# Routed experts on one Trainium2 core: TensorE's order written out unit by unit

## The chip, the cores and the metric

One NeuronCore of a Trainium2 chip runs the whole program. The metric is the device time of one execution in microseconds (us), as the median of several runs; smaller is better. TensorE does the matrix products, VectorE (DVE) and ScalarE (ACT) the elementwise work, GpSimd (POOL) some of it, and SyncE (SP) issues the loads from HBM.

## The reference

The program is a two-layer transformer block followed by a second block with a retention mixer, a delta-rule mixer and a mixture of experts, for 256 tokens of 1024 features in float32. The change is in the last stage alone, the routed experts. Each token picks 8 of 64 experts; expert `e` computes

```
(silu(x @ w_gate[e]) * (x @ w_up[e])) @ w_down[e]        # 1024 -> 256 -> 1024
```

for the tokens that picked it. The outputs, each times its token's weight, are added up per token, the shared expert's output is added, and the sum is normalised and added to x.

## The kernel before

**Units and groups.** The experts are ordered by load. The first 12 places get 128 slots for tokens each, the next 28 get 64, the last 24 get 32 (`TIERS`, L53). A unit is 128 slots: one expert, two or four. A group is two units, 256 slots. There are 16 groups, so 32 units: 12 of one expert, 14 of two, 6 of four. `ORDER` (L55) gives the tiers of the groups: 0, 2, 0, 0, 1, 1, 0, 1, 1, 0, 1, 2, 0, 1, 1, 2. Numbered from 0, units 2, 3, 22, 23, 30 and 31 have four experts, units 0, 1, 4 to 7, 12, 13, 18, 19, 24 and 25 have one.

**What a group and a unit do.** `gather` (L1742) picks a group's tokens with one-hot matrices: one step on VectorE and ScalarE (the one-hot tile `oh` and its bfloat16 copy `ohb`), then four steps of 8 matmul records each (`pm<-oh,tok`), each copied by ScalarE into the tile `xg` (2 buffers). A unit's gate and up products (`pd<-ring,xg`) come in four chunks; chunk `c` uses one tile of weights per expert (128 x 1024 floats, 512 KB). Every float32 product is two records. With one expert the records are 128*128, the whole array; with two or four they are 128*64 or 128*32, so that two or four experts stand side by side in the array's columns (column-tiled). A chunk is 4, 8 or 16 records. After that come the steps of `tail` (L1830): `onehot` (products `pm<-slT,idb` and `pm<-w,ohb`; VectorE makes from them `PT`, the matrix that brings outputs back to tokens, and `wc`, the slots' weights); `act` (`swiglu`, L1873: tanh on ScalarE, three steps on VectorE, the last writes `h`); `trans` (two transposes of `h`, L1858, copied by ScalarE into `hT`); two `down` steps (`pm<-ring,hT`, 4, 8 or 16 records each, column-tiled like gate and up), each split by ScalarE and VectorE into the two parts of `y` (3 buffers). Per group `scatter` (L1892) adds four steps of 4 records (`pm<-y,PT`, whole array), each added to the sum `macc` by VectorE (L1883).

**Weights.** `ring` (L1573) loads each tile of weights on SP's queue into one of 25 buffers (`NRING`, L50). An expert takes 6 loads: 4 of `w_gu`, 2 of `w_ed`. A unit of one, two or four experts takes 6, 12 or 24, the routed experts take 384, and the shared expert's last product takes 2 more beside group 2 (`SHD`, L52; products `pm<-ring,hs`, 16 records). A load waits until a buffer is free, that is until the products of an earlier tile are done.

**Order.** Python issues a chunk of gate and up products, then one or two (four experts: up to three) calls of `pump` (L1786), each of which issues one step of `tail` and one of `gather`. This is the order of priority only. The framework's scheduler, working from its own estimate of times when the program is built, decides the final order on each engine, and on TensorE it may put any product that is ready in front of another. PSUM has three `pd` buffers and four `pm` buffers (L329, L332). `final_rows` (L1954) runs beside the last group; it makes rows for the last norm, and holds one `y` and one `xg` buffer from then on.

Of the kernel before, what the change touches and what calls it, by code (L numbers as in the profile page):

```python
# [28 lines left out]
# ----------------------------------------------------------------- constants (of the shapes alone)  # L29
# [24 lines left out]
# the tiers of the groups of 256 slots, in the order in which they are taken  # L54
# [6 lines left out]
def _consts():  # L61
# [3 lines left out]
    # additive masks, queries on partitions  # L65
# [4 lines left out]
    # [partition t, free i]  # L70
# [4 lines left out]
    # within 32 rows and columns, lower and upper: the second block of a pair of s rows, the first of s columns  # L75
# [30 lines left out]
    # rope rows: 0..31 cos, 32..63 sin (with the sign), twice  # L106
# [40 lines left out]
def _layout(inp):  # L147
# [50 lines left out]
    # second block  # L198
# [34 lines left out]
# ----------------------------------------------------------------- kernel  # L233


class Kern:
# [12 lines left out]
    # -------- streams of instructions: generators that yield where another stream may come in  # L249
# [35 lines left out]
    def mm3(self, out, L, R, n, start=True, stop=True):  # L285
        """out = sum over n k-tiles of L[k]^T R[k]; L, R: (hi, lo) callables of k"""
# [19 lines left out]
    def split(self, hi, lo, src, lo_eng=None):  # L306
        """hi + lo = src exactly, each with at most 12 significant bits"""
# [3 lines left out]
    def wraw(self, src, n):  # L311
        """src [128, n] in DRAM, loaded"""
# [6 lines left out]
    def wload(self, src, n, pre=True):  # L319
        """src [128, n] in DRAM -> hi, lo [128, n]"""  # L320
# [25 lines left out]
    # -------- setup  # L346
# [67 lines left out]
    def t5_bias(self, tp):  # L414
        """bias tiles [128 q, 8 heads, keys] with the masks added"""
# [5 lines left out]
        # differences of neighbouring buckets; bucket 0 keeps its value  # L421
# [4 lines left out]
        # three exact bf16 parts, block-diagonal over the key groups  # L426
# [26 lines left out]
                # ps columns (k, g, h) -> bias[q, h, g * nk + h0 + k]  # L453
# [6 lines left out]
    # -------- 1/sqrt(src * scale + eps), [128, n] for small n  # L460
# [13 lines left out]
    def rows(self, cols, dst):  # L474
        """dst [128, 256] = cols [128, 2] (tokens on partitions) as a row on every partition"""
# [6 lines left out]
    def rstd(self, sqs, n, name, dst=None):  # L482
        """1/sqrt(mean + eps) over the partitions of the [128, 256] tiles sqs: (columns [128, 2], rows [128, 256])"""
# [7 lines left out]
    def rstd_rows(self, sqs, n, tmp):  # L491
        """rows of 1/sqrt(mean + eps) over the partitions, worked out on every partition; tmp [128, 4, 256]"""
# [5 lines left out]
    def add_sq(self, acc, k, x, eng=None, **kw):  # L498
        """acc (+)= x^2, the first k writing it"""
# [10 lines left out]
    # -------- dense products; activations (hi, lo) [128, KT, 256]; calls cb(f, psum [128, n * 256], n)  # L510
# [97 lines left out]
            # output projection (the gates' halves come in here), residual  # L608
# [13 lines left out]
    def ff(self, l, XM, r, fp, res):  # L622
        """x += mlp(x), in two halves of the hidden features; res: the next XG and sums of squares"""
# [31 lines left out]
    def queries(self, l, XG, r, qp):  # L655
        """projections of the sliding-window attention"""
# [22 lines left out]
    def mixer(self, l, XG, Q, mp):  # L679
# [4 lines left out]
        # convolution branch: GLU, then the taps  # L684
# [20 lines left out]
        # sliding-window attention  # L705
# [9 lines left out]
        # latent attention: projections and norms of the latents  # L715
# [25 lines left out]
        # gates (tanh: 2 * sigmoid - 1) and the gated sum of the branches, which takes the first gate's place  # L741
# [15 lines left out]
        def branch(n, Y, f, gate):  # L757
            """outputs f, f + 1 of branch n"""
# [11 lines left out]
        # latent attention  # L770
# [50 lines left out]
        # layer norm over channels, swish  # L821
# [32 lines left out]
    def residual(self, k, X, g, acc, eng=None):  # L854
        """after x^T tile k is final: hi, lo of x*g and its part of the sum of squares"""
# [6 lines left out]
    # ---------------------------------------------------------------- second block  # L862
# [11 lines left out]
    def modulation(self, js, mp):  # L874
        """stream: parts js of the modulation, as columns [128, 8] each; 0, 1 for the context too (columns 48..63)"""
# [39 lines left out]
    def modulated(self, x, r, a, b, X, pool):  # L915
        """hi, lo of x * r * a + b; r rows, a and b columns per k-tile"""
# [6 lines left out]
    def decays(self, pool):  # L923
        """powers of the retention's decays: columns"""
# [8 lines left out]
    def decay_tables(self, pool):  # L933
        """DT [128 j, 4, 128 i], both directions; rows of powers"""
# [14 lines left out]
    def tr4(self, dst, srcs, scale=None):  # L949
        """dst [128, 4, 128] = transposes of four [128, 128] tiles, times scale(i) [128, 1]"""  # L950
# [11 lines left out]
    def rope2(self, dst, ps, f, scale, pool):  # L962
        """dst [128, 2, 256] = rotated ps (two heads), times scale"""
# [8 lines left out]
    def short_conv(self, z, ps, tile0, pool):  # L972
        """z [128, 2, 256] = 2 * silu(conv(ps)) of two channel tiles"""
# [12 lines left out]
    def l2(self, zs, pool, kt, ktok, mul):  # L986
        """z = 2 * silu; kt [128, 4, 256] (channels on partitions) and ktok [128, 2, 4, 128] of the normalised heads, times mul"""
# [12 lines left out]
    def state_features(self, X, base, pool, rope, F):  # L1000
        """stream: the features that feed the states, into the dict F"""
# [27 lines left out]
        # the decay gates first  # L1029
# [14 lines left out]
    def gdn_gates(self, p3, la, be, pool):  # L1044
        """la = -exp(a_log) * softplus(p + dt_bias), be = sigmoid(p)"""
# [6 lines left out]
        # softplus(x) = max(x, 0) + log1p(exp(-|x|)); log1p(e) = 2 atanh(e / (2 + e))  # L1052
# [23 lines left out]
    def retention_kv(self, F, d, n, pool, kv):  # L1076
        """kv [PSUM 128 d, (4, 128 e)] of chunk n, direction d"""
# [989 lines left out]
```

## Time and profile before

| what | value |
|---|---|
| median of 3 runs | 2062.32 us (2062.28 to 2063.19) |
| span of the profiled execution | 2062.9 us |
| TensorE busy / VectorE / ScalarE | 92% / 62% / 38% of the span |
| granted TensorE clock, mean | 0.951 of full speed |
| routed experts' first and last product of a ring tile | 1458.2 and 2048.0 us |
| loads of the ring | 390 of 512 KB |

The profiled execution's own time is its span, 0.6 us above the median of the runs, so the two can be used side by side. A row of a timeline merges neighbouring records of one kind; its time runs from the first start to the last end. Matmuls are pipelined: one record of 512 columns shows some 600 ns from start to end while the next one has long begun. What a run costs is therefore read from the start of one row to the start of the next. Records that work in different columns of the array overlap fully.

### The profile page before, as it was taken

Reading aid. Unit: us, or ns where it says so; the run is one execution under the profiler, and the core shown is the slowest. Engines: PE = TensorE matmul, PEld = TensorE weight load, DVE = VectorE, ACT = ScalarE, POOL = GpSimd, SP = SyncE. Lnnn points to the kernel's source line nnn. Section 1 sums busy time; section 2 is a strip of 40 time slices with the busy share of each in tenths; the row PEclk is TensorE's granted clock in tenths of the full one; section 3 lists DMA queues with packets and bytes.
Section 4 is the critical chain, followed back from the end, with each engine's and each line's share of the span. In section 5 each row is a group of like instructions: output and inputs, shape, how many; then the busy total and the mean of one; then the engine's idle time right before and its main releaser. Section 6 shows DMA issues by size and latency. Waiting matters only on the chain. (4 is left out here: it accounts for less than half of the span.)

```text
span 2062.9 us, 38136 instructions
## 1 busy us (share of the span) xinstructions
PE 1900.5 (92%) x15189; PEld 1512.5 (73%) x15189; DVE 1272.2 (62%) x2464; ACT 786.7 (38%) x1397; POOL 292.4 (14%) x216
## 2 busy tenths in 40 slices
PE   5888999999888999998988998996999999999996
PEld 5787999999787999998987988895645443433432
DVE  7999787887986688578657864487222222222223
ACT  3246555344257555444444433352212121121111
POOL 3433210001334220011131121103000000000000
PEclk9989999999989999999989997896999999999998
DMA  4423556776423567655523522154798988889994
GB/s 160 124 82 113 171 177 201 244 245 200 134 76 106 176 202 228 210 172 172 156 91 96 161 91 65 33 180 186 264 409 305 353 276 304 283 287 409 348 349 197
DMA packets 122149, 414.49 MB, mean 201 GB/s; under 512 B 13936, under 2 KB 14832, under 8 KB 121968
## 3 DMA queue, kind: packets, MB, share of 16 engines
q1 hardware_dynamic: 120528, 409.92, 58.7%
q8 instruction: 120, 1.97, 0.4%
q10 hardware_dynamic: 1440, 2.11, 0.3%
q14 instruction: 61, 0.50, 0.1%
HBM read 410.92 MB, written 1.05 MB: 200 GB/s over the span
## 5 line engine op out<-in xcount | busy, mean ns | idle before, releaser
L283 PE MATMUL pd<-X,whi 128*128 128x256 f32 (+2 forms) x3280 | 639.3, 294 | 19.6 <-DVE X L304 9.8
L283 PEld LDWEIGHTS pd<-X,whi 128*128 128x128 f32 (+2 forms) x3280 | 534.0, 198 | 25.9 <-DVE X L304 11.7
L292 ACT ACTIVATE whi<-raw 128x1024 fp32r<-128x1024 f32 x340 | 356.4, 1051 | 458.7 <-PE pd L283 341.2
L283 PE MATMUL pd<-X,wlo 128*128 128x256 f32 (+2 forms) x1640 | 480.0, 293 | 8.2 <-POOL wlo L295 4.6
L295 DVE TENSOR_TENSOR wlo<-raw,whi 128x1024 fp32r<-128x1024 f32 x286 | 357.5, 1253 | 130.7 <-ACT whi L292 125.7
L283 PEld LDWEIGHTS pd<-X,wlo 128*128 128x128 f32 (+2 forms) x1640 | 324.7, 198 | 12.2 <-POOL wlo L295 6.1
L283 PE MATMUL pd<-ring,xg 128*64 128x512 f32 (+2 forms) x1024 | 284.3, 602 | 0.0
L283 PE MATMUL pd<-H,whi 128*128 128x256 f32 x1024 | 188.4, 286 | 0.3 <-ACT H L292 0.3
L295 DVE TENSOR_TENSOR y<-pm,y 128x512 fp32r<-128x512 f32 x64 | 44.2, 691 | 209.6 <-ACT y L292 209.5
L283 PEld LDWEIGHTS pd<-ring,xg 128*64 128x64 f32 (+2 forms) x1024 | 78.3, 136 | 113.4 <-issue 105.3
L295 POOL TENSOR_TENSOR wlo<-raw,whi 128x1024 fp32r<-128x1024 f32 (+1 forms) x54 | 132.6, 2470 | 197.6 <-ACT whi L292 197.2
L283 PEld LDWEIGHTS pd<-H,whi 128*128 128x128 f32 x1024 | 159.4, 192 | 1.1 <-ACT H L292 0.5
L283 PE MATMUL pm<-ring,hT 128*64 128x512 f32 (+2 forms) x512 | 153.7, 601 | 1.6 <-ACT hT L292 1.6
L304 DVE SCALAR_TENSOR_TENSOR cv<-up,vec,cv 128x256 f32<-128x256 f32 x240 | 148.1, 656 | 0.2
L283 PE MATMUL pd<-H,wlo 128*128 128x256 f32 x512 | 145.2, 284 | 0.4 <-DVE wlo L295 0.4
L304 DVE SCALAR_TENSOR_TENSOR acc<-rawm,sl,acc 128x512 f32<-128x512 f32 x112 | 94.1, 855 | 22.6 <-DMA rawm<-in_w_mod 22.2
L292 ACT ACTIVATE y<-pm 128x512 fp32r<-128x512 f32 (+1 forms) x66 | 39.4, 597 | 171.4 <-PE pm L283 171.4
L283 PEld LDWEIGHTS pd<-H,wlo 128*128 128x128 f32 x512 | 98.1, 192 | 0.8 <-DVE wlo L295 0.8
L283 PEld LDWEIGHTS pm<-ring,hT 128*64 128x64 f32 (+2 forms) x512 | 42.1, 136 | 75.1 <-issue 66.8
L283 PEld LDWEIGHTS pm<-oh,tok 128*128 128x128 f32 x512 | 67.2, 189 | 35.0 <-issue 29.3
L295 POOL TENSOR_TENSOR sqacc<-sqacc,sq 128x256 f32<-128x256 f32 x42 | 37.7, 905 | 366.0 <-ACT sq L292 364.9
L283 PE MATMUL pm<-oh,tok 128*128 128x256 f32 x512 | 87.3, 306 | 1.8 <-DVE oh L295 1.8
(515 smaller groups left out, 2721.6 us busy)
## 6 DMA issues: line engine op xcount, KB each, us to landing
ring<-in_w_gu SPq DMA_DIRECT2D x256, 512.0 KB, 6.8
ring<-in_w_ed SPq DMA_DIRECT2D x128, 512.0 KB, 8.5
raw<-in_w_up SPq DMA_DIRECT2D x64, 512.0 KB, 4.3
raw<-in_w_dn SPq DMA_DIRECT2D x64, 512.0 KB, 4.3
raw<-in_w_g SPq DMA_DIRECT2D x48, 512.0 KB, 3.6
rawm<-in_w_mod SPq DMA_DIRECT2D x96, 256.0 KB, 3.5
raw<-in_w_s SPq DMA_DIRECT2D x32, 512.0 KB, 3.7
raw<-in_w_x SPq DMA_DIRECT2D x32, 512.0 KB, 3.5
```

The costliest lines, as they stand in the source:

```text
L283: return self.nc.tensor.matmul(out, l, r, start=start, stop=stop)
L292: self.nc.scalar.activation(out, in_, f, **kw)
L295: (eng or self.nc.vector).tensor_tensor(out, a, b, op)
L304: self.nc.vector.scalar_tensor_tensor(out, a, s, b, op0, op1)
```

## The change

`experts` gets a new loop, and `tail` is taken apart into methods of the same content (`slots`, `hidden`, `turn`, `down`). The scheduler is told that TensorE's instructions keep the order in which Python issues them (`manual_schedule`); the other engines and SP's queue are scheduled as before. Of each unit first all gate and up products are issued, then what uses the whole array (two steps of the next group's gather, the next unit's `slots`, this unit's transposes, two steps of an earlier group's scatter, each with a step of the shared expert or of `final_rows` if there is one), then the unit's two down products. `slots` moves one unit ahead of where `onehot` stood, and `PT` gets a fifth buffer for that. `final_rows` starts with the last group but one. The remaining hunks take comments and docstrings out; the line numbers stay nearly the same.

```diff
     def experts(self, first):
...
-        nxt = self.gather(*order[0])
-        todo.extend(nxt[1])
-        for g, (j0, n) in enumerate(order):
-            while todo:
-                todo.popleft()()
-            if g == SHD:
-                tail.extend(first)
-            if g == len(order) - 1:
-                tail.extend(self.final_rows())
...
-                for c in range(4):
-                    ws = [self.expert_w("w_gu", self.expert(U, i), c) for i in range(nu)]
-                    for kk in range(2):
...
-                    pump()
-                    if nu == 1 or c % 2:
-                        pump()
-                    if nu == 4:
-                        pump()
-                tail.extend(self.tail(U))
...
+        with self.tc.manual_schedule(engines={mybir.EngineType.PE}):
+            st, steps = self.gather(*groups[0])
+            for f in steps:
+                f()
...
+            group(0, st)
+            self.slots(units[0])
+            for i in range(2 * len(groups)):
+                U = units[i]
+                g, second = divmod(i, 2)
+                if not second and g + 1 < len(groups):
+                    st, steps = self.gather(*groups[g + 1])
+                    group(g + 1, st)
+                    todo.extend(steps)
+                if i == 2 * SHD:
+                    extra.extend(first)
+                if i == 2 * len(groups) - 4:
+                    extra.extend(self.final_rows())
+                self.gate_up(U)
+                self.hidden(U)
+                for _ in range(2 if second else 3):
+                    if todo:
+                        todo.popleft()()
+                if i + 1 < len(units):
+                    self.slots(units[i + 1])
+                self.turn(U)
+                for _ in range(2):
+                    if out:
+                        out.popleft()()
+                    if extra:
+                        extra.popleft()()
+                for hf in range(2):
+                    self.down(U, hf)
+                if second:
+                    out.extend(self.scatter(units[i - 1:i + 1]))
+            while out:
+                out.popleft()()
...
-    def tail(self, U):
...
-            U["PT"] = mp.tile([P, S], F32R, name="PT", tag="PT", bufs=4)
...
+    def slots(self, U):
...
+        U["PT"] = mp.tile([P, S], F32R, name="PT", tag="PT", bufs=5)
```

## Rows read from the trace of the kernel before

**Rows 1.** The page: busy time of TensorE, share of the span, instructions.

```profile
PE 1900.5 (92%) x15189; PEld 1512.5 (73%) x15189; DVE 1272.2 (62%) x2464; ACT 786.7 (38%) x1397; POOL 292.4 (14%) x216
```

**Rows 2.** By window: us; PE, PEld, DVE, ACT, POOL busy; granted clock, DMA share, GB/s.

```profile
1866.00:1920.00 54.00, 52.07 (x236) 20.37 (x234) 14.11 (x34) 8.79 (x17) 0.00 (x0) 1.00 1.03 409
...
1993.00:2036.00 43.00, 38.96 (x230) 14.47 (x227) 12.00 (x30) 7.78 (x15) 0.00 (x0) 1.00 0.97 383
...
1458.00:2049.00 591.00, 581.38 (x2639) 247.65 (x2638) 158.10 (x347) 112.25 (x216) 0.00 (x0) 1.00 0.87 321
```

**Rows 3.** Timeline of TensorE, one two-expert unit: start, us, line, out<-in, records.

```profile
1606.40 1.94 PE L283 MATMUL pd<-ring,xg 128*64 128x512 f32 x8
1608.27 1.20 PE L283 MATMUL pm<-y,PT 128*128 128x512 f32 x4
1609.40 1.94 PE L283 MATMUL pd<-ring,xg 128*64 128x512 f32 x8
1611.27 2.14 PE L283 MATMUL pm<-y,PT 128*128 128x512 f32 x8
1613.33 1.94 PE L283 MATMUL pd<-ring,xg 128*64 128x512 f32 x8
1615.20 0.30 PE L283 MATMUL pm<-slT,idb 64*64 64x256 bf16 x2
1615.43 1.07 PE L283 MATMUL pd<-ring,xg 128*64 128x512 f32 x2
1616.43 0.30 PE L283 MATMUL pm<-w,ohb 128*128 128x2 bf16 x6
1616.66 1.94 PE L283 MATMUL pd<-ring,xg 128*64 128x512 f32 x8
1618.53 0.44 PE L1858 MATMUL pm<-cst,h 128*128 128x128 f32 x2
1618.90 1.50 PE L283 MATMUL pd<-ring,xg 128*64 128x512 f32 x5
```

**Rows 4.** The same timeline: two column-tiled runs, one behind the other.

```profile
1636.61 1.89 PE L283 MATMUL pd<-ring,xg 128*64 128x512 f32 x8
1638.33 1.89 PE L283 MATMUL pm<-ring,hT 128*64 128x512 f32 x8
```

**Rows 5.** Timeline of TensorE, the first group: whole-array products.

```profile
1454.36 3.99 PE L283 MATMUL pm<-oh,tok 128*128 128x256 f32 x32 [1.81 <-DVE oh L295]
1458.18 1.88 PE L283 MATMUL pd<-ring,xg 128*128 128x512 f32 x4
...
1474.90 3.60 PE L283 MATMUL pm<-ring,hT 128*128 128x512 f32 x8
1478.33 1.88 PE L283 MATMUL pd<-ring,xg 128*128 128x512 f32 x4
```

**Rows 6.** Timeline of ScalarE and VectorE: one unit from sums to hidden features.

```profile
1516.89 0.38 ACT L292 ACTIVATE tg<-pd 128x256 f32<-128x256 f32 x1 [2.84 <-PE pd L283]
...
1518.15 0.42 DVE L295 TENSOR_TENSOR h<-tg,pd 128x256 f32<-128x256 f32 x1
...
1520.80 0.39 ACT L292 ACTIVATE hT<-pm 128x256 f32<-128x256 f32 x1 [3.04 <-PE pm L1858]
```

**Rows 7.** Ring tiles: ns min/median/max; idle until (us, times); landing of loads, us.

```profile
L283 PE MATMUL pd<-y,ring x64: 379/379/792, 1428.2 to 1452.2; 128*128 128x256 f32 x64
...
  DMA ring<-in_w_gu: 1.1, 2
...
DMA to landing us min/median/max: 3.5/7.2/12.2
```

**Rows 8.** Timeline of all engines, the end of the last unit.

```profile
2046.68 1.90 PE L283 MATMUL pm<-ring,hT 128*32 128x512 f32 x10
...
2048.62 0.60 ACT L292 ACTIVATE y<-pm 128x512 fp32r<-128x512 f32 x1 [4.59 <-PE pm L283]
2049.25 0.69 DVE L295 TENSOR_TENSOR y<-pm,y 128x512 fp32r<-128x512 f32 x1 [2.67 <-ACT y L292]
```

More of the change, by code (lines that the diff above doesn't have):

```diff
@@ L1780, in experts @@
         tiers = [list(range(a, b, 256 // n)) for (a, n), b in zip(TIERS, [t[0] for t in TIERS[1:]] + [NE])]
-        order = []
+        groups = []
         for i in ORDER:
-            order.append((tiers[i].pop(0), 256 // TIERS[i][1]))
-        todo, tail, pend = deque(), deque(), []
-        def pump():
-            if tail:
-                tail.popleft()()
-            if todo:
-                todo.popleft()()
-        nxt = self.gather(*order[0])
-        todo.extend(nxt[1])
-        for g, (j0, n) in enumerate(order):
-            while todo:
-                todo.popleft()()
-            if g == SHD:
-                tail.extend(first)
-            if g == len(order) - 1:
-                tail.extend(self.final_rows())
-            st = nxt[0]
-            if g + 1 < len(order):
-                nxt = self.gather(*order[g + 1])
-                todo.extend(nxt[1])
-            nu = n // 2
-            for u in range(2):
-                U = {"js": list(range(j0 + u * nu, j0 + (u + 1) * nu)), "st": st, "s0": u * P, "reg": {}, "ps": self.pd()}
-                m = P // nu
-                for c in range(4):
-                    ws = [self.expert_w("w_gu", self.expert(U, i), c) for i in range(nu)]
-                    for kk in range(2):
-                        k = 2 * c + kk
-                        for i, w in enumerate(ws):
-                            s0 = U["s0"] + i * m
-                            self.mm(U["ps"][i * m:(i + 1) * m], st["x"][:, k, s0:s0 + m], w[:, kk * 512:(kk + 1) * 512], k == 0, k == KD - 1)
-                    pump()
-                    if nu == 1 or c % 2:
-                        pump()
-                    if nu == 4:
-                        pump()
-                tail.extend(self.tail(U))
-                pend.append(U)
-                if len(pend) == 2:
-                    tail.extend(self.scatter(pend))
-                    pend = []
@@ L1825, in experts, with group @@
-        while tail:
-            tail.popleft()()
+            groups.append((tiers[i].pop(0), 256 // TIERS[i][1]))
+        with self.tc.manual_schedule(engines={mybir.EngineType.PE}):
+            st, steps = self.gather(*groups[0])
+            for f in steps:
+                f()
+            units = []
+            todo, extra, out = deque(), deque(), deque()
+            def group(g, st):
+                j0, n = groups[g]
+                nu = n // 2
+                for u in range(2):
+                    units.append({"js": list(range(j0 + u * nu, j0 + (u + 1) * nu)), "st": st, "s0": u * P, "reg": {}})
+            group(0, st)
[30 more added lines that the diff above has]
+                out.popleft()()
@@ L1827, in experts, with gate_up @@
         self.o = self.xg().rearrange("p (t k) s -> p t (k s)", t=2)
         self.norm_out()
-    def tail(self, U):
+    def gate_up(self, U):
+        U["ps"] = self.pd()
+        n = len(U["js"])
+        m = P // n
+        for c in range(4):
+            ws = [self.expert_w("w_gu", self.expert(U, i), c) for i in range(n)]
+            for kk in range(2):
+                k = 2 * c + kk
+                for i, w in enumerate(ws):
+                    s0 = U["s0"] + i * m
+                    self.mm(U["ps"][i * m:(i + 1) * m], U["st"]["x"][:, k, s0:s0 + m], w[:, kk * 512:(kk + 1) * 512], k == 0, k == KD - 1)
@@ L1832, in tail @@
+    def slots(self, U):
         nc, mp, n = self.nc, self.mb, len(U["js"])
         m = P // n
-        def onehot():
-            ps = self.pm()
-            j = U["js"][0]
-            for i in range(n):
-                self.mm(ps[i * m:(i + 1) * m, 0:S], self.idb[:, j + i:j + i + 1].to_broadcast([NE, m]), self.slT, True, True)
-            U["PT"] = mp.tile([P, S], F32R, name="PT", tag="PT", bufs=4)
-            c = {1: 1, 2: 2, 4: 7}[n]
-            self.ts(U["PT"], ps[:, 0:S], self.c("cols")[:, c:c + 1], ALU.is_equal)
-            q = ps[:, S:S + n]
-            for i in range(3):
-                for t in range(2):
-                    self.mm(q, U["st"]["Pb"][:, t, U["s0"]:U["s0"] + P], self.w3[:, i, t, j:j + n], i == 0 and t == 0, i == 2 and t == 1)
-            U["w"] = mp.tile([P, 1], F32, name="wc", tag="wc", bufs=3)
-            for i in range(n):
-                r = slice(i * m, (i + 1) * m)
-                nc.vector.tensor_copy(U["w"][r], q[r, i:i + 1])
@@ L1852, in act @@
-        def act():
-            U["h"] = self.swiglu(U["ps"], U["w"])
-        def trans():
-            ps = self.pm()
-            for k in range(2):
-                nc.tensor.transpose(ps[:, k * P:(k + 1) * P], U["h"][:, k * P:(k + 1) * P], self.ident)
-            U["hT"] = mp.tile([P, 2, P], F32, name="hT", tag="hT", bufs=2)
-            self.act(U["hT"].rearrange("p k s -> p (k s)"), ps[:, 0:S], AF.Copy)
-            U["y"] = self.y()
-        def down(hf):
-            yp = self.pm()
-            ws = [self.expert_w("w_ed", self.expert(U, i), hf) for i in range(n)]
-            for k in range(2):
-                for i, w in enumerate(ws):
-                    self.mm(yp[i * m:(i + 1) * m], U["hT"][:, k, i * m:(i + 1) * m], w[:, k * 512:(k + 1) * 512], k == 0, k == 1)
-            o = slice(hf * 512, (hf + 1) * 512)
-            self.split(U["y"][:, 0, o], U["y"][:, 1, o], yp)
@@ L1871, in tail @@
-        return [onehot, act, trans] + [lambda hf=hf: down(hf) for hf in range(2)]
+        ps = self.pm()
+        j = U["js"][0]
+        for i in range(n):
+            self.mm(ps[i * m:(i + 1) * m, 0:S], self.idb[:, j + i:j + i + 1].to_broadcast([NE, m]), self.slT, True, True)
+        U["PT"] = mp.tile([P, S], F32R, name="PT", tag="PT", bufs=5)
+        c = {1: 1, 2: 2, 4: 7}[n]
+        self.ts(U["PT"], ps[:, 0:S], self.c("cols")[:, c:c + 1], ALU.is_equal)
+        q = ps[:, S:S + n]
+        for i in range(3):
+            for t in range(2):
+                self.mm(q, U["st"]["Pb"][:, t, U["s0"]:U["s0"] + P], self.w3[:, i, t, j:j + n], i == 0 and t == 0, i == 2 and t == 1)
@@ new lines, in slots, with hidden, turn @@
+        U["w"] = mp.tile([P, 1], F32, name="wc", tag="wc", bufs=3)
+        for i in range(n):
+            r = slice(i * m, (i + 1) * m)
+            nc.vector.tensor_copy(U["w"][r], q[r, i:i + 1])
+    def hidden(self, U):
+        U["h"] = self.swiglu(U["ps"], U["w"])
+    def turn(self, U):
+        ps = self.pm()
+        for k in range(2):
+            self.nc.tensor.transpose(ps[:, k * P:(k + 1) * P], U["h"][:, k * P:(k + 1) * P], self.ident)
+        U["hT"] = self.mb.tile([P, 2, P], F32, name="hT", tag="hT", bufs=2)
+        self.act(U["hT"].rearrange("p k s -> p (k s)"), ps[:, 0:S], AF.Copy)
@@ new lines, in down @@
+    def down(self, U, hf):
+        n = len(U["js"])
+        m = P // n
+        if hf == 0:
+            U["y"] = self.y()
+        yp = self.pm()
+        ws = [self.expert_w("w_ed", self.expert(U, i), hf) for i in range(n)]
+        for k in range(2):
+            for i, w in enumerate(ws):
+                self.mm(yp[i * m:(i + 1) * m], U["hT"][:, k, i * m:(i + 1) * m], w[:, k * 512:(k + 1) * 512], k == 0, k == 1)
+        o = slice(hf * 512, (hf + 1) * 512)
+        self.split(U["y"][:, 0, o], U["y"][:, 1, o], yp)
```

## The prediction

> **What bounds the kernel now.** I read four views, in this order. The page says that TensorE is busy for 92% of the span [rows 1], so time can only come off what TensorE does. The windows say that the experts' stage is even fuller: 581.4 of 591 us, at the full granted clock, with the DMA engines at 321 GB/s [rows 2]. In one window of the same stage they move 409 GB/s, so over the stage loads are no tight bound yet, and TensorE was idle for a `w_gu` tile for 1.1 us in all [rows 7]. The timeline shows what the busy time is made of. Four chunks of one two-expert unit take from 1606.40 to 1618.5, though two runs of 8 column-tiled records that touch follow each other in 1.72 us [rows 3, 4], so four need 6.88. Between the chunks stand scatter, `slots` and transposes, and each change between column-tiled and whole-array products leaves part of the array empty. A busy row hides this. In one place 2 records, a quarter of a run and worth 0.43 us, hold the engine for 1.00 before `w,ohb` starts [rows 3], since only one of the array's two halves has work. The stage is bound by the order on TensorE, not by its products.
>
> **Prices of TensorE's work.** All are from start to start.
> - Column-tiled run, next to another one: 1.72 [rows 4]. In front of whole-array work 1.87 [rows 3], so leaving costs 0.15.
> - Scatter: 4 records take 1.13, 8 take 2.06 up to the next tiled run [rows 3]. That is 0.2325 a record and 0.20 for coming back.
> - Whole-array float32 record: 3.43 for 8, 0.429 [rows 5].
> - Gather: 3.82 for 32 records [rows 5], 0.119; I take 1.0 for a step of 8.
> - `slots` and transposes: 0.23, 0.23 and 0.37 between tiled runs [rows 3]. These hold 0.15 to 0.2 of switching each, which is counted already, so I take 0.6 for the three, between 0.3 and 0.83.
>
> **The change part by part.** *Order within a unit.* No product, load or elementwise step is added or removed. A unit becomes: gate and up, two gather steps, next unit's `slots`, transposes, two scatter steps, two downs. For two or four experts that is 4x1.72 + 0.15 + 2.0 + 0.6 + 8x0.2325 + 0.20 + 2x1.72 = 15.13 us; for one expert 16x0.429 + 2.0 + 0.6 + 1.86 + 8x0.429 = 14.75. Units 0 and 1 have no scatter (1.86 less each), and unit 4 has the shared expert's 16 records (6.86).
>
> *New waits on TensorE.* With its order fixed, whatever waits holds all behind it. The transposes wait for `h`; behind them stand scatter, the downs and the next unit. From tanh to the end of `h` takes 1.68 us (1516.89 to 1518.57) [rows 6]; with some 0.35 around it, 2.0. In front of the transposes stand 0.15 + 2.0 + 0.4, so half a microsecond is left. Without this cover it would cost 2.0 a unit. The downs wait for `hT`, 0.39 on ScalarE [rows 6], behind 1.86 of scatter. The gather needs `oh`, two VectorE steps that depend on nothing of the unit and fit into the 6.9 us of gate and up; if VectorE took them after `h`, a group's first unit would lose 3. I allow 0.2 us a unit for what collides. Queued behind the unit's steps on VectorE are `PT` and the sums, which nothing needs before the next unit.
>
> *SP's queue.* Loads of `w_ed` go ahead of the next unit's `w_gu`, with the same 25 buffers and 386 loads. GpSimd does nothing in this stage [rows 2]. A load is 524,288 bytes, 1.282 us at 409 GB/s and 1.369 at 383 [rows 2]. I take 1.30, nearer to the window without a ragged end. The shortest way from issue to landing is 3.5 [rows 7].
>
> *`PT`'s fifth buffer* costs nothing but space. *`final_rows`* now takes one `y` and one `xg` buffer in unit 28. So the last gather can't be copied before unit 29's gate and up are done, two of four `pm` buffers stay taken, and `y` of unit 28 waits for unit 29's scatter. I put this at up to 8 us in units 28 and 29; the loads of units 30 and 31, below, hide it. Uncovered it costs those 8.
>
> **The sum.** The first expert product starts at 1458.2 [rows 5]; `slots` ahead of it makes that 1458.6. Units 0 to 21 are 10 of one expert and 12 others: 147.5 + 181.6 - 3.7 + 6.9 = 332.2. Within them unit 3 starves. When unit 2 starts at 1484.4, 37 loads have landed and unit 3's last is number 60. The first buffer comes free at 1486.1; 3.5 + 22x1.30 later, 1518.2, number 60 lands, and its run ends at 1519.9 against 1514.7 without the wait: 5.2. Unit 22 then starts at 1458.6 + 332.2 + 5.2 = 1796.0. One-expert units (7.8 us of loads in 14.75) have refilled the ring by then, and two-expert units (15.6 in 15.13) hardly drain it. From here loads are the bound. 230 are used up, 25 are in the ring, 131 remain. They follow one another from 1797.7: 3.5 + 130x1.30 gives 1970.2 for the last. TensorE alone would need 150 us for units 22 to 31 and be done by 1946, so 24 us of waiting in units 23, 30 and 31 cover any stall in this half. The last run ends at 1972.0.
>
> The tail behind the last down product is now 14.3 us (2048.58 to 2062.9) [rows 8]. After the change, three of four scatter steps stand behind it, the second waiting 1.4 for ScalarE and VectorE [rows 8], then 3x4x0.2325: 4.2 in place of 2.1, a tail of 16.4. Two more for a slower clock after the waits of unit 31, and 0.2 for each of units 2 to 21: 1972.0 + 16.4 + 2 + 4 = **1994**. The span before is 0.6 us over the median of the runs, which is less than what I can resolve; I forecast 1994 us, 3.3% less.
>
> By the Trainium skill, HBM Reference, Specifications, a core is to expect about 358 GB/s. The window at 409 disagrees [rows 2], and the row decides. By 358 a load would take 1.46, and the sum, an estimate from that page, would be some 2018.
>
> **Rivals.** *The hidden chain is exposed.* VectorE's order is still the scheduler's. If it puts `PT` of the next unit ahead of this unit's steps, the transposes come 2.0 later, and `oh` behind `h` costs 3 in a group's first unit: 2.5 a unit on average. Units 0 to 21 get 55 longer, less the starving of unit 3: 1994 - 4 + 50 = 2040. For it: only TensorE's order is written out, and nothing in the trace fixes VectorE's. Against it: VectorE and ScalarE are busy for 158 and 112 of 591 us [rows 2], so a step that is ready seldom finds them taken.
>
> *The clock falls where loads are late.* At the lower of the two levels a record takes twice as long (792 against 379 ns) [rows 7]. Runs that wait for loads hide that, but what follows in unit 3 (some 8 us) and at the end (1.7 and 3.7 for the last run and scatter) does not: 1994 - 2 + 13 = 2005. The Trainium skill, TensorE: Matmul & The Clock Gate, HAM oscillation, warns of just this pattern, bursts between waits for loads. Here the clock stood at 1.00 in the window of 43 us in which loads were late before [rows 2], so I give it little.
>
> *Nothing is gained*, 2062: the empty parts of the array are an artefact of how records are drawn, and a stage busy for 98% stays so. By the Trainium skill, Perfetto Trace Analysis, Identifying the Most-Contended Engine, matmul busy time doesn't tell the distance to the limit. The starts in rows 3 and 4, not the busy time, bear the gain.
>
> *Slower: the ring loses its lead.* Loads issue in order on SP and each waits for a buffer. If the scheduler's own estimate hands out buffers in another order than TensorE frees them, a load at the head waits for a late buffer, all behind it too, and TensorE can no longer put other work into the gap. With no lead each unit costs the larger of its work and its loads: 6x31.2 + 14x15.6 + 12x14.75 + 6.9 = 589.5, an end at 1458.6 + 589.5 + 16.4 = 2064.5. It decides from there: any wait at a unit's first load, up to 3.5, comes on top, with half of 32x3.5 some 2120. Against it: buffers are handed out in the order of the units, and that is now TensorE's order too.
>
> **How the numbers follow.** The forecast reaches from 1973 (no allowances, 6 less; `slots` and transposes at 0.3, 6; loads at 1.282, 3; no cost of coming back and gather at 0.119 a record, 6, all over some 20 units) to 2010 (loads at 1.369, 11; `slots` and transposes at 0.83, 5). It gets 0.66. The exposed chain gets 0.18, the clock 0.08, no gain 0.03, slower 0.05. The range 1973 to 2030 takes in the forecast, the clock and the milder half of the exposed chain, 0.66 + 0.08 + 0.09 = 0.83. Faster by over 0.2% (4.1 us, about what a measurement of this kernel can tell) is 0.66 + 0.18 + 0.08 = 0.92, no change 0.03, slower 0.05.
>
> **What would show it.** Right: each unit of two or four experts is one row of tiled products, then whole-array rows, then downs; a unit outside the starved ones takes 15.1 or 14.8 from start to start; unit 22 starts near 1796 to 1800; loads run at some 409 GB/s from there; idle time for ring tiles is tens of us, in units 3, 23, 30 and 31. Wrong: idle time in front of the transposes or of `oh,tok` in most units (the chain), a granted clock under 1 within the stage, or waits for ring tiles in two-expert units before unit 22 (the ring).

## The result, and the profile after

The changed kernel takes 2013.18 us in the median of three runs (2005.18 to 2023.58), the kernel before 2062.30 in the same comparison: a ratio of 0.9757, with a 95% interval of 0.9717 to 0.9797. A fourth run was a slow one, of 5998.98 us, and is left out; with it the median on record is 2018.38. The time lies in the range of the prediction, 19 us above its forecast of 1994 (24 by the median on record). The profiled execution was the longest of the three and has a span of 2021.7. Its page shows TensorE less busy than before [rows 1], by 65.8 us:

```profile
PE 1834.7 (91%) x15189; PEld 1517.0 (75%) x15189; DVE 1275.9 (63%) x2464; ACT 787.3 (39%) x1397; POOL 292.8 (14%) x216
```

The number of records is the same, so nothing that the kernel computes went away. The windows of the experts' stage, to be read like [rows 2], show two halves that differ:

```profile
1465.00:1825.00 360.00, 343.12 (x1667) 171.98 (x1670) 108.80 (x237) 77.03 (x147) 0.00 (x0) 1.00 0.88 329
1825.00:2005.00 180.00, 165.97 (x960) 74.73 (x960) 48.21 (x105) 34.00 (x65) 0.00 (x0) 1.00 1.00 396
...
1900.00:1960.00 60.00, 56.75 (x324) 29.34 (x320) 16.04 (x38) 13.20 (x26) 0.00 (x0) 1.00 1.03 409
...
2005.00:2021.00 16.00, 4.30 (x17) 2.92 (x16) 10.86 (x39) 3.49 (x9) 0.00 (x0) 0.75 0.18 68
```

Up to unit 22 (at 1824.9) loads move 329 GB/s and are no bound but in unit 3; from there they run at 396 to 409 and TensorE waits for them. It is busy for 166.0 of 180 us. Of the 14.0 in which it stands, its waits put 3.9 down to loads, 5.5 to `PT` and 3.4 to `h`; most of the waiting for loads hides in rows that show as busy, as is seen below.

The granted clock shows as 1.00 in both halves because it is a mean. It is 1.00 from 1825 to the tail, but in unit 0 it fell to the lower of its two levels, 0.50 or 1.2 GHz, for 3.4 us. A window of just that stretch, and TensorE's row of unit 0's down products:

```profile
1477.10:1480.50 3.40, 3.40 (x5) 1.35 (x4) 0.00 (x0) 0.36 (x1) 0.00 (x0) 0.50 0.00 1
```

```profile
1476.67 5.40 PE L283 MATMUL pm<-ring,hT 128*128 128x512 f32 x8 [0.76 <-ACT hT L292]
```

Just before, TensorE had waited 0.58 us for `PT` and 0.76 for `hT`. The same 8 records take 3.70 in a run below in which the clock stayed up, so this cost 1.7 us.

TensorE's timeline shows one two-expert unit in the written order, gate and up in one row, then what uses the whole array, then the downs, and the next unit's first row:

```profile
1603.93 7.09 PE L283 MATMUL pd<-ring,xg 128*64 128x512 f32 x32
1610.94 2.14 PE L283 MATMUL pm<-oh,tok 128*128 128x256 f32 x16
1613.02 0.30 PE L283 MATMUL pm<-slT,idb 64*64 64x256 bf16 x2
1613.89 0.29 PE L283 MATMUL pm<-w,ohb 128*128 128x2 bf16 x6 [0.58 <-DVE PT L300]
1614.05 0.41 PE L1871 MATMUL pm<-cst,h 128*128 128x128 f32 x2
1614.22 2.10 PE L283 MATMUL pm<-y,PT 128*128 128x512 f32 x8
1616.25 3.65 PE L283 MATMUL pm<-ring,hT 128*64 128x512 f32 x16
1619.74 1.03 PE L283 MATMUL pd<-ring,xg 128*64 128x512 f32 x4
```

From start to start that is 15.81 us. In [rows 3] the four chunks alone, with scatter and `slots` between them, took 12.1 (1606.40 to 1618.53), before any transpose or down product. Counted on TensorE's timeline of the stage, the column-tiled products of the kernel before stand in 146 runs, 82 of them of fewer than 8 records; after the change in 25, none of them short.

One wait is new in nearly every unit: in front of `w,ohb` TensorE stands 0.58 us here until VectorE has made `PT`. The waits of TensorE from 1450 to 2010 show it once for each of the 32 units, 0.63 us on average; the columns are the total in us, the times and the longest:

```profile
PE pm L283 <- DVE PT L300: 20.2, 32, 0.8
PE pd L283 <- DMA ring<-in_w_gu: 4.3, 15, 0.9
PE pm L1871 <- DVE h L295: 3.4, 2, 1.8
```

The idle time for ring tiles, of weight loads into the array and of products together, was 1.1 us for `w_gu` before [rows 7]. It is now as follows for the whole run, and behind the dots stands the landing of the loads issued after 1824:

```profile
  DMA ring<-in_w_gu: 30.1, 51
  DMA ring<-in_w_ed: 8.5, 19
...
DMA to landing us min/median/max: 7.0/10.1/11.1
```

These waits are where the prediction put them, in units 3, 23 and 31 (22.75, 24.47 and 24.90 us long). Most are short pieces between two loads, as in unit 23 on TensorE's timeline:

```profile
1840.73 4.49 PE L283 MATMUL pd<-ring,xg 128*32 128x512 f32 x34
1845.45 1.04 PE L283 MATMUL pd<-ring,xg 128*32 128x512 f32 x2 [0.23 <-DMA ring<-in_w_gu]
1846.73 1.04 PE L283 MATMUL pd<-ring,xg 128*32 128x512 f32 x2 [0.23 <-DMA ring<-in_w_gu]
```

The two rows of 2 records are 1.28 us apart, which is one load. A row of 2 records is worth 0.22 us and shows 1.04 busy, so a busy share hides most of such a wait. At the end of TensorE's timeline all four steps of the last scatter, 16 records, follow the last downs (before, the last 4 records did):

```profile
2003.47 1.90 PE L283 MATMUL pm<-ring,hT 128*32 128x512 f32 x10 [0.22 <-DMA ring<-in_w_ed]
...
2005.31 3.99 PE L283 MATMUL pm<-y,PT 128*128 128x512 f32 x16
```

### The profile page after: what moved, and what is told of

Read it like the earlier page. It is cut to its first block, busy times and chain, and to the rows that moved or that the text cites. A ratio compares the mean times of both kernels' runs of the same rounds, so it can differ in the third digit from the quotient of the medians.

```text
span 2021.7 us, 38128 instructions
## 1 busy us (share of the span) xinstructions
PE 1834.7 (91%) x15189; PEld 1517.0 (75%) x15189; DVE 1275.9 (63%) x2464; ACT 787.3 (39%) x1397; POOL 292.8 (14%) x216
## 4 chain that ended last, share of the span: by engine, by line
PE 51%; DVE 10%; DMA 5%; issue 4%; POOL 2%; ACT 2%; POOLq 0%; DVEq 0%; SPq 0%; ACTq 0%
PE pd L283 31%; PE pm L283 18%; DMA ring<-in_w_gu 2%; DVE wlo L295 2%; DMA ring<-in_w_ed 2%; DVE cv L304 2%; POOL wlo L295 1%; DMA rawm<-in_w_mod 1%; ACT whi L292 1%; DVE sm L304 1%; DVE PT L300 1%; PE pm L953 1%; DVE iY L295 0%; PE pst L283 0%; PE pm L1871 0%
## 5 line engine op out<-in xcount | busy, mean ns | idle before, releaser
L292 ACT ACTIVATE whi<-raw 128x1024 fp32r<-128x1024 f32 x340 | 356.4, 1051 | 462.4 <-PE pd L283 343.5
L283 PE MATMUL pd<-ring,xg 128*64 128x512 f32 (+2 forms) x1024 | 242.0, 594 | 4.3 <-DMA ring<-in_w_gu 4.3
L304 DVE SCALAR_TENSOR_TENSOR cv<-up,vec,cv 128x256 f32<-128x256 f32 x240 | 152.2, 673 | 0.2
L304 DVE SCALAR_TENSOR_TENSOR tg<-tg,pd 128x256 f32<-128x256 f32 x32 | 13.5, 421 | 218.0 <-ACT tg L292 218.0
L283 PE MATMUL pm<-ring,hT 128*64 128x512 f32 (+2 forms) x512 | 122.2, 601 | 2.4 <-ACT hT L292 1.2
L304 DVE SCALAR_TENSOR_TENSOR acc<-rawm,sl,acc 128x512 f32<-128x512 f32 x112 | 94.0, 854 | 24.5 <-DMA rawm<-in_w_mod 24.1
L292 ACT ACTIVATE tg<-pd 128x256 f32<-128x256 f32 x32 | 12.3, 384 | 231.5 <-PE pd L283 231.5
```

Source lines behind the costliest of these rows:

```text
L283: return self.nc.tensor.matmul(out, l, r, start=start, stop=stop)
L292: self.nc.scalar.activation(out, in_, f, **kw)
L304: self.nc.vector.scalar_tensor_tensor(out, a, s, b, op0, op1)
```

## The experiments

The ten runs below are compared with the kernel before, run on the same chip. Times of whole runs carry the part of the program ahead of the experts, which varies, so "the stage" stands beside them: from the start of the first expert product to the end of the span in the one profiled execution. It is 604.7 us before and 556.1 after. The first unit's `slots` stand ahead of this start in the new text and behind it in the old, which favours the new text by up to 1.5 us.

**The changed kernel again.** No edit.

> The changed kernel once more, as it is, for the runs beside it. The code ahead of the experts' stage runs in the same order on TensorE before and after the change, so a first expert product at 1465.5 us, 7 later than before, is partly chance: I expect 1455 to 1466 this time, and from there to the end of the span 556 us, within 5. If the change itself delays the earlier stages, it is 1465 again.

2013.88 us, ratio 0.9752 [0.9725, 0.9780]; first expert product at 1456.3, stage 554.9. The first expert product had been at 1465.5 in the first profile. What stands ahead of it on TensorE is the same list of instructions in the same order as before, so those 9 us between two executions of one kernel are variation of the earlier stages. In these two profiles the stage agrees within 1.2 us; it is the measure for the rest. Unit 0's 3.4 us at the lower clock are there again.

**The comparison last.** In `slots` the step that writes `PT` moves behind the six `w,ohb` records.

```diff
-        self.ts(U["PT"], ps[:, 0:S], self.c("cols")[:, c:c + 1], ALU.is_equal)
         q = ps[:, S:S + n]
         for i in range(3):
...
+        self.ts(U["PT"], ps[:, 0:S], self.c("cols")[:, c:c + 1], ALU.is_equal)
```

> VectorE's comparison that makes PT is put behind the six small products with the weights, in the same PSUM buffer. Theory: TensorE stands still 0.6 us in every unit because these products wait for the comparison; the wait goes, a unit outside the starved ones takes 15.2 (two or four experts) and 14.8 us (one) in place of 15.8 and 15.5, the units up to 21 gain 13 us and the load-bound rest starts that much earlier: 12 to 14 us less than the changed kernel from the first expert product to the end. Rival: the transposes then wait for h instead (1.1 to 1.4 us lie between h and them now, so 0.5 should be left); then units stay at 15.8 and nothing is gained.

1996.64 us, ratio 0.9689 [0.9666, 0.9712]; stage 541.1, 15.0 less than after. TensorE's timeline of a two-expert unit:

```profile
1614.06 7.04 PE L283 MATMUL pd<-ring,xg 128*64 128x512 f32 x32
1621.03 2.15 PE L283 MATMUL pm<-oh,tok 128*128 128x256 f32 x16
1623.11 0.30 PE L283 MATMUL pm<-slT,idb 64*64 64x256 bf16 x2
1623.34 0.30 PE L283 MATMUL pm<-w,ohb 128*128 128x2 bf16 x6
1623.50 0.42 PE L1871 MATMUL pm<-cst,h 128*128 128x128 f32 x2
1623.67 2.10 PE L283 MATMUL pm<-y,PT 128*128 128x512 f32 x8
1625.71 3.65 PE L283 MATMUL pm<-ring,hT 128*64 128x512 f32 x16
1629.19 7.04 PE L283 MATMUL pd<-ring,xg 128*64 128x512 f32 x32
```

From `slT` to scatter it is 0.56 us (1623.11 to 1623.67) instead of 1.20 (1613.02 to 1614.22), and the unit takes 15.13. The wait is thus shown, with its place: `w,ohb` writes other columns of the PSUM buffer that the comparison reads, and no value passes from one to the other. Why the framework lets the one wait for the other, for the buffer's sake or the bank's, is not shown. Units 0 to 21 take 343.5 us instead of 359.4. Of these 15.9, 14 are the 0.63 of 22 units, and 1.7 came with unit 0, where the clock stayed at 1.00 this time. From unit 22 on loads bind, and what TensorE saves there it waits for loads: unit 31 grows from 24.9 to 27.7. In unit 30 the clock fell to 0.50 for 3.4 us (from 1941.2), behind a wait of 2.33 for `h`.

**The order not fixed.** The new text, with the scheduler free on TensorE as before.

```diff
-        with self.tc.manual_schedule(engines={mybir.EngineType.PE}):
+        with ExitStack():
```

> The changed kernel without the fixed order on TensorE: the same program text, the scheduler free as before the change. Theory: the gain comes from unbroken runs, and the scheduler breaks them again: 2040 to 2065 us. Rival: the new order of the text is enough, since it also sets the priorities: within 10 us of the changed kernel, some 2010.

2031.93 us, ratio 0.9855 [0.9830, 0.9879]; stage 576.5. Neither expectation held whole. In most units the scheduler keeps the written runs, and it avoids the wait for `PT` by taking the transposes first. In six two-expert units (16, 17, 21 and 27 to 29) and in five of the six four-expert units it breaks runs as before; here in unit 22, on TensorE's timeline:

```profile
1813.16 1.04 PE L283 MATMUL pd<-ring,xg 128*32 128x512 f32 x2
1814.13 0.86 PE L283 MATMUL pm<-oh,tok 128*128 128x256 f32 x5
1814.93 1.04 PE L283 MATMUL pd<-ring,xg 128*32 128x512 f32 x2
1815.90 1.58 PE L283 MATMUL pm<-oh,tok 128*128 128x256 f32 x11
```

Two records, worth 2/16 of 1.72 or 0.22 us, hold TensorE for 0.97. The stage has 68 tiled runs, 31 of them short, 20 of these in two-expert units. And the transposes, called too early, wait for `h` 12 times, by TensorE's waits:

```profile
PE pm L1871 <- DVE h L295: 21.4, 12, 1.9
```

**Half of `w_ed`.** Half of the bytes of the down weights is loaded; the number of products stays.

```diff
-        ws = [self.expert_w("w_ed", self.expert(U, i), hf) for i in range(n)]
+        ws = [self.expert_w("w_ed", self.expert(U, i), hf, 512) for i in range(n)]
...
-                self.mm(yp[i * m:(i + 1) * m], U["hT"][:, k, i * m:(i + 1) * m], w[:, k * 512:(k + 1) * 512], k == 0, k == 1)
+                self.mm(yp[i * m:(i + 1) * m], U["hT"][:, k, i * m:(i + 1) * m], w[:, 0:512], k == 0, k == 1)
```

> Each load of w_ed brings half of its columns (256 KB), and both halves of the down products use that half, so the down products' second half of the features is left out and the first used twice; the products' number and shapes stay. Theory: units 3, 23, 30 and 31 wait for loads, and from unit 22 the loads set the end; with a sixth of the bytes gone the waits shrink, 10 to 20 us less from the first expert product to the end. Rival: TensorE's own order sets the end everywhere; within 3 us of the changed kernel.

2000.21 us, ratio 0.9705 [0.9679, 0.9732]; stage 544.9, 11.2 less than after. Unit 31 falls from 24.9 to 18.7 and unit 23 from 24.5 to 21.5. From unit 22 to the end of the span it is 189.1 instead of 196.8 us, so 7.7 of the 11.2 come from there: loads bind the second half of the stage. Of the rest, 1.8 come from unit 3, which waits less for loads, and 1.7 from unit 0, where the clock stayed at 1.00. That last part is not shown to be a gain of the edit.

**The old text, its order fixed.** The loop of the kernel before, unchanged, with TensorE in the order in which Python issues it.

```diff
+        with self.tc.manual_schedule(engines={mybir.EngineType.PE}):
             nxt = self.gather(*order[0])
...
             while tail:
                 tail.popleft()()
```

> The kernel before with its own loop, but with TensorE's order fixed to that of the text (a chunk of gate and up, a step of the tail, a step of the gather, and so on). Theory: no run is broken in the middle, but each unit of two or four experts still goes in and out of column-tiled runs four or five times in place of once, 0.35 us each, and the transposes and downs come one step after what they wait for: some 2 us more a unit than the changed kernel, 575 to 600 us from the first expert product to the end of the span (604.7 before, 555 changed). Rival: unbroken runs are all of the gain, then 550 to 562.

2018.33 us, ratio 0.9765 [0.9736, 0.9793]; stage 559.7. The theory fell, the rival held: with none of the new text, only 3.6 us of the 48.6 are missing, and by whole runs (0.9765 against 0.9752 for the changed kernel run again) the two can't be told apart. TensorE still changes between tiled and whole-array work several times a unit:

```profile
1602.73 1.94 PE L283 MATMUL pd<-ring,xg 128*64 128x512 f32 x8
1604.60 1.20 PE L283 MATMUL pm<-y,PT 128*128 128x512 f32 x4
1605.73 1.94 PE L283 MATMUL pd<-ring,xg 128*64 128x512 f32 x8
...
1611.53 0.30 PE L283 MATMUL pm<-slT,idb 64*64 64x256 bf16 x2
1612.41 0.29 PE L283 MATMUL pm<-w,ohb 128*128 128x2 bf16 x6 [0.58 <-DVE PT L300]
```

But none of its 89 tiled runs is shorter than a chunk, so no chunk is broken. In the kernel before, by an estimate from the trace, the 82 short runs held TensorE for 108 us, and their records were worth 56 at 1.72 for a full run. So 64 changes more than after, at the 0.35 a pair that the prediction used (22 us), seemed to cost next to nothing. The ring's idle time and a window say why:

```profile
  DMA ring<-in_w_ed: 3.4, 9
  DMA ring<-in_w_gu: 2.7, 8
```

```profile
1860.00:1900.00 40.00, 38.47 (x185) 19.44 (x183) 10.46 (x21) 9.02 (x17) 0.00 (x0) 1.00 1.03 408
```

Loads run at the same 408 GB/s as after, and the last one lands 541 us behind the first expert product (in the changed kernel 538). But TensorE hardly waits for them: its extra work lies in time in which the changed kernel waits. If that is so, the new text must show its worth once loads bind less. The run of the old text with the comparison last and the new groups, below, tests it.

**Another order of the groups**, on top of the comparison last: four-expert groups no longer close to each other, nor at the end.

```diff
-ORDER = (0, 2, 0, 0, 1, 1, 0, 1, 1, 0, 1, 2, 0, 1, 1, 2)
+ORDER = (0, 1, 2, 0, 1, 1, 1, 1, 0, 2, 0, 1, 0, 1, 2, 0)
```

> The changed kernel with the comparison put last, and with another order of the groups: 0, 1, 2, 0, 1, 1, 1, 1, 0, 2, 0, 1, 0, 1, 2, 0. The groups of four experts, 48 loads each, come at places 2, 9 and 14 in place of 1, 11 and 15, and a group of single experts ends the stage. Same products, same loads. Theory: the loads set the end from unit 22 because 48 loads stand at the very end; with 12 there, the last load lands some 15 us before the last down product, and the waits for loads fall from some 30 to some 15 us: 524 to 532 us from the first expert product to the end (541.1 with the old order of groups). Rival: the loads are bound as a whole, since 386 of 1.30 us make 502; then nothing is gained, 538 to 544.

1985.79 us, ratio 0.9635 [0.9615, 0.9655]; stage 528.7, as expected. It has the lowest time here, 3.65% under the kernel before. In twelve units, 6 to 17, TensorE is busy without a gap:

```profile
1555.00:1736.00 181.00, 181.00 (x892) 90.93 (x895) 60.66 (x131) 41.20 (x79) 0.00 (x0) 1.00 1.02 406
```

**`final_rows` with the last group**, on top of the comparison last; in the last two units three of its steps go out instead of two.

```diff
-                if i == 2 * len(groups) - 4:
+                if i == 2 * len(groups) - 2:
...
-                for _ in range(2):
+                for _ in range(3 if i >= 2 * len(groups) - 2 else 2):
```

> The changed kernel with the comparison put last, and with the rows of the last norm taken up beside the last group again, in place of the last but one. Theory: units 28 and 29 lose their extra 1.8 and 3.2 us and take 15.1 each, and units 30 and 31 wait that much longer for loads: 541 us from the first expert product to the end, within 2. Rival: TensorE's own work counts there too, 536.

1994.47 us, ratio 0.9657 [0.9635, 0.9679]; stage 540.9 against 541.1. Units 28 and 29 fall from 16.9 and 18.3 to 15.1 and 15.2, units 30 and 31 grow from 18.0 and 27.7 to 21.7 and 28.4. The cost of `final_rows` was real, 4.9 us, and hidden behind loads, as predicted.

**Both of these edits together.**

> The other order of the groups and the rows of the last norm beside the last group. Theory: with the last groups bound by TensorE, the 5 us that these rows cost two units earlier are no longer covered by waits for loads: 1 to 5 us less than with the order of the groups alone. Rival: no difference, if the four-expert group at place 14 still waits for its loads.

1992.76 us, ratio 0.9642 [0.9614, 0.9670]; stage 531.5, so 2.8 more than with the groups alone where 1 to 5 less was expected. A miss. Unit 28 falls to 15.2, but unit 29 takes 25.1 and unit 30 18.1: the four-expert unit 29 waits for loads all the longer (24.3 with the groups alone), and the rows themselves now lie in unit 30 (15.8 with the groups alone). The intervals of the two overlap, so that it is slower isn't shown; that it gains, as expected, isn't either.

**The old text fixed, with the comparison last and the new groups.**

> The old text with TensorE's order fixed, and now with both later edits, the comparison last and the other order of groups, so that loads bind less. Stage means from the first expert product to the end of the span. Theory (the unbroken runs are the gain, and where the whole-array work stands between them is worth little; its places between the chunks even fill waits for loads): 526 to 536, as the new text with both edits, 528.7. Rival (the new text gathers the whole-array work once a unit, which saves three or four changes of 0.35 us a unit; behind late loads that did not show, and now it does): 540 to 552.

1997.06 us, ratio 0.9699 [0.9664, 0.9733]; stage 542.3. The theory fell again, and the time is the rival's: behind the new text with the same edits, 528.7, it is 13.6 us late. In units 6 to 17 no product waits for a load, and they take 185.7 us against 180.7 with the new text. Loads run at the same 406 GB/s, and TensorE has more to do:

```profile
1540.00:1726.00 186.00, 184.35 (x898) 85.59 (x890) 55.63 (x124) 40.40 (x76) 0.00 (x0) 1.00 1.02 406
```

The rival's reason covers only part of the 13.6. The old text starts `final_rows` with the last group; the new text with these rows there, the run of both edits above, took 531.5, so 10.8 is the fairer difference. Also, the last two units take 47.3 us in the old text, from unit 30's first product to the last down product, and 30.4 in the new, because the old puts each unit's down products and scatter off into the next and has them, with `final_rows`, to do at the end. How the difference divides between the changes of tiling and this end is not shown beyond the 5.0 us of units 6 to 17.

**The kernel before, with both edits.**

> The kernel before, TensorE's order still the scheduler's, with the comparison last and the other order of groups. Theory (before, TensorE's broken runs are the bound; it hardly waits for loads or for the comparison): a stage of 598 to 606, against 604.7 before. Rival (the two edits gain by themselves, whoever orders TensorE): 575 to 590, some 13 for the comparison and some 10 for the groups.

2060.75 us, ratio 0.9985 [0.9961, 1.0008]; stage 606.2. The theory held: without the fixed order the edits bring nothing. TensorE's timeline shows broken runs in a two-expert unit:

```profile
1609.50 1.20 PE L283 MATMUL pm<-y,PT 128*128 128x512 f32 x4
1610.63 1.07 PE L283 MATMUL pd<-ring,xg 128*64 128x512 f32 x2
1611.63 0.50 PE L283 MATMUL pm<-y,PT 128*128 128x512 f32 x1
1612.07 1.93 PE L283 MATMUL pd<-ring,xg 128*64 128x512 f32 x6
```

Eight records in two pieces cost 1.00 and 1.86, where 1.72 to 1.87 would do. Of its 138 tiled runs 73 are short. The stages side by side:

| TensorE's order | comparison first, old groups | comparison last, new groups |
|---|---|---|
| the scheduler's, old text | 604.7 | 606.2 |
| the scheduler's, new text | 576.5 | not run |
| fixed, old text | 559.7 | 542.3 |
| fixed, new text | 556.1 | 528.7 |

## Why the prediction was right, and where it was not

**The reason was right, but only its first half carried the gain.** The prediction said that the stage is bound by TensorE's order, with two costs: broken runs, and many changes between tiled and whole-array work. Of the 48.6 us that the stage gained, 45.0 come with a fixed order alone, which ends the broken runs. The rest of the new text, above all that it gathers the whole-array work in one place, brought 3.6, since loads bound the second half; it is worth 10.8 to 13.6 once they bind less, of which 5.0 are shown in units that wait for no load.

**The prices of TensorE's work were right, but for one.** Predicted were 15.13 us for a two-expert unit and 14.75 for a one-expert unit; with the comparison last they are 15.13 to 15.23 and 14.76 to 14.91. The changed kernel takes 15.8 to 16.0 and 15.4 to 15.65. The term that failed is **`slots` and transposes, taken as 0.6** "between 0.3 and 0.83": they take 1.20. The prediction read 0.23 from the rows of `slT` and `w,ohb` and took the 2 tiled records between them, which held TensorE for 1.00, for waste [rows 3]. They were also the cover of a wait. VectorE's timeline of the kernel before shows `PT` in just that stretch:

```profile
1615.54 0.48 DVE L300 TENSOR_SCALAR PT<-pm,cst 128x256 fp32r<-128x256 f32 x1 [1.41 <-PE pm L283]
```

The scheduler had put other work there nearly always: by the waits of TensorE in the stage of the kernel before, only two units waited.

```profile
PE pm L283 <- DVE PT L300: 1.3, 2, 0.7
```

A written order that puts `slT` and `w,ohb` next to each other takes this cover away. The prediction said of `PT` that nothing needs it before the next unit, which is true of its values, not of the buffer that it reads. The Trainium skill, PSUM — Partial Sum Buffer, section PSUM bank collisions raise a hardware error, says that accesses are to be kept apart by bank and quadrant, not by address; the wait of 0.58 us between disjoint columns agrees, and this rule would have led to the term.

**The sum, closed.** From 1994 to the span of 2021.7: the first expert product came 6.9 us late (1465.5 for 1458.6). Of this 5.8 stand in the stages ahead of the experts and vary by chance, as the repeated run shows; 1.1 are mostly the first unit's `slots`, whose wait for `PT` was not allowed for. Units 0 to 21 took 359.4 instead of 341.4 with the allowance: 18 more, 14 of which are the wait for `PT` and 1.7 the lower clock in unit 0. From unit 22 to the last landing it was 178.5 instead of 174.2. The period of loads was right, 1.29 for 1.30, but the first load issued there landed 7.7 us behind the start of unit 22, where the prediction had 1.7 for a buffer and 3.5, the shortest row, for the landing; and 133 loads were still to be issued, not 131. Four others were in flight. In that stretch no load landed in less than 7.0, and the shortest way was the wrong row. The tail was right: the last run ended 1.9 after the last landing (predicted 1.8), and 16.4 followed (predicted 16.4, by luck in part: with three steps of scatter and a wait of 1.4, where four steps came and no wait). The 2 us for a slower clock in unit 31 did not come. Together 6.9 + 18.0 + 4.3 - 1.9 is 27.3. With the comparison last and the wait gone the span is 1992.6, near the forecast, but a start at 1451.5 helps: from the first expert product on, 535.4 was forecast and 541.1 came.

**By its other steps.** *The hidden chain* stayed covered: half a microsecond was thought to be left; with the `PT` wait gone `h` ends 0.5 to 0.7 ahead of the transposes. TensorE waited for `h` only in units 30 and 31, which have no gather left as a cover: 1.61 and 1.77 us, near the 2.0 that this was priced at. Units 0 and 1, which have no scatter, waited 0.76 and 0.47 for `hT`; the prediction had no term for that. *The last of the ring:* unit 3 starved by 6.9 us (predicted 5.2); waits stood in units 3, 23 and 31, as said (unit 30, named too, hardly waited), and no two-expert unit before unit 22 waited. *`final_rows`* cost 1.7 and 2.6 in units 28 and 29, within its 8, and loads hid it. *The clock* stayed at 1.00 in units 3 and 31, where loads were late, so that rival failed in this kernel. (In the run with `final_rows` beside the last group it did fall in unit 3, for 3.4 us behind a wait of 1.56 for a load.) The 1.7 us that the lower level did cost stood in unit 0, which no part of the prediction named. *By the share of 358 GB/s* the sum came to 2018, nearer to the measured time than the forecast, and for the wrong reason: loads moved 408 and 409. The Trainium skill, HBM Reference, Specifications, goes on to say that a core streaming alone measures about 425, well over its share; the measured 409 agrees with this sentence, which the prediction should have taken, not with the one it did take.

## What to carry to other kernels

When a scheduler's order is replaced by a written one, go through each pair of instructions that the new order makes neighbours, and ask what stood between them and what wait it covered; a filler that looks like waste may be a cover. On TensorE, first make sure that column-tiled runs are not broken, since pieces of two records cost 2.3 to 4.5 times their worth here; gathering whole-array work came second here, and paid where TensorE, not the loads, was the bound. Count a gain stage by stage: what is saved where loads bind comes back as waiting.

## What the runs showed that was not expected

- A product that writes 1 to 4 columns of a PSUM buffer waits for a VectorE read of 256 other columns of the same buffer, 0.63 us on average in each of 32 units, 20.2 us in all.
- The stages ahead of the experts, with TensorE's instructions in the same order, give way to the first expert product anywhere between 1446.5 and 1465.5 us in the profiles of this study, which are from several chips; the experts' stage of the changed kernel agreed within 1.2 us in its two profiles.
- From unit 22 on, with pieces of waiting for loads of mostly 0.2 us and two waits for `h` of 1.61 and 1.77, the granted clock of the changed kernel stayed at 1.00 up to the tail, where it fell to 0.50 (0.75 on average) and TensorE was busy for 4.3 of 16 us. In unit 0 it fell for 3.4 us behind waits of 0.58 and 0.76, in both profiles of this kernel. With the comparison last it fell for 3.4 us in unit 30, behind a wait of 2.33. What decides between these cases is not shown.
